# The gates' second products, two pairs behind their first, in a hybrid pooling and attention block

## The chip, the cores and the metric

The kernel runs on one core of one Trainium2 chip. Its time is the device time of one execution in microseconds (us). Before the change it is 1161.26 us, the median of 3 runs (1159.54 to 1161.93). One more execution was profiled; it took 1161.2 us, and its records span 1159.4 us. Engines are named as in the profile: PE is TensorE (PEld its weight loads), DVE VectorE, ACT ScalarE, POOL GpSimd, SP SyncE, which here only issues transfers (DMAs).

## The reference

One decoder block on x of 1024 tokens by 1024 channels, float32:

```
h = rmsnorm(x, g_mix_pre);  proj = h @ w_in + b_in
u_pool, q, k, v, gates = split(proj)            # 512, 512, 128, 128, 2 x 1024
# pooling mixer: 4 groups of 128 channels, windows 2, 4, 8, 16
y_pool = (mean of u over the last w tokens - u) @ w_pool[group] * pool_scale
# attention: 8 query heads on 2 key heads, blocks of 128 tokens, window 128, one sink logit a head
y_attn = softmax([q k^T / 8, sink]) v
merged = sigmoid(gates[:1024]) * (y_pool @ w_branch_pool) + sigmoid(gates[1024:]) * (y_attn @ w_branch_attn)
x = x + rmsnorm(merged @ w_out, g_mix_post)
ff = square(relu(rmsnorm(x, g_mlp_pre) @ w_up)) @ w_down
x = x + rmsnorm(ff, g_mlp_post)
```

## The kernel before, in words

**Products.** A float32 product is made of three matmuls of rounded halves: each operand is split into a high part (a cast, L101, on ScalarE) and the rest (a subtraction, L104, on VectorE); `split` does both. A `wh` tile holds such a split weight; there are six buffers of them (`wp`). A raw weight comes into a `st` buffer (three of them, 512 KB a load).

**Attention.** Tokens are cut into 8 blocks. The loop over n works on three blocks at a time: `attend_t(n)` transposes the probabilities of block n on TensorE, the softmax of block n+1 is finished, the scores of block n+2 are made (`score`, copied out of PSUM by ScalarE at L329; `score_prev` puts the previous block's scores in by VectorE at L336). `attend_v(n)` multiplies with v; its result is copied out by ScalarE at L392. `fill` puts matmuls of other work between: the rest of the q, k, v projection and then the pooling projection u (L576), groups 3, 2, 1, 0, in two halves each. VectorE scales each half (L579); ScalarE adds the bias when both are there (L582). The order of TensorE, VectorE and ScalarE in this loop is the order in which the code is written.

**Pooling.** `pool_in(gi)` makes the windowed mean of group gi on VectorE, in steps that the caller takes one by one: each doubling of the window is an add of shifted tiles (L605) and a short copy (L606); then the difference to u (L609 and two short rows, L610, L611); then a split into `ar` tiles. `pool_mix(gi)` is six matmuls (L624 to L626) in two `at` banks of PSUM; in the attention there are three such banks, which `attend_t` (two each) and `attend_v` use too.

**Gates.** The gate projection, 16 tiles of 128 channels, is computed pair by pair (8 pairs) with a Strassen-Winograd scheme: of 2x2 blocks (two channel tiles, two halves of the tokens) only 7 products are made instead of 8, each of 4 k-tiles and 3 passes, 12 matmuls (L480). `m1(p)` makes the first product in a bank `mm` (there are four) and has ScalarE copy the bank (L487); `m2(p)` accumulates the second product onto the same bank, and VectorE closes it (L718). Neither needs more than the x tiles of the attention stage. `rest(p)` makes the other five (names b6, b7, b5, and two that go into these banks again) and closes the two gate tiles: sigmoid on ScalarE, then out to DRAM (`z_dram`). These need tiles made from differences of x: `build_gate(kt)`, kt 0 to 3, loads two x tiles (L744, SyncE's queue), scales one on ScalarE (L746), makes four differences on VectorE (L749 to L752) and splits them (four casts, four subtractions). `prepare(p)` loads the raw weights of pair p and splits the two that m1 and m2 need; `operand(p, i)` makes the other five.

Behind the attention, before: for pairs 0 to 6 m1 and m2 are made one after the other, with pool_mix(2), (1), (0) and the four build_gate between; pairs 5 and 6 put their result (`f0`) to DRAM and get it back ahead of their rest(p); pair 7 makes its first two products inside rest(7). In this part only TensorE's order is the written one; where the other engines' rows stand is decided by a scheduler. The engines' queues, and SyncE's queue of transfers, are each worked off in order.

## Time and profile before

| | us |
|---|---|
| median of 3 runs | 1161.26 (1159.54 to 1161.93) |
| the profiled execution | 1161.2, span 1159.4 |
| TensorE busy, whole span | 1126.5 (97%) |
| VectorE, ScalarE busy | 821.2 (71%), 526.6 (45%) |
| TensorE busy from 165 to 235 us | 55.3 of 70 |

In the profile, L12 is line 12 of the kernel before. A row of the timeline reads: start in us, duration in us, engine, line, operation, output<-inputs, shape, how many, and in brackets how long the engine was idle before, and what ended that. ACTq and SPq rows are issues of transfers. A share of busy time over the whole span says little here: TensorE is full in all but two stages, the start and the one behind the attention, so the prediction goes by stages.

### The profile page before, as it was taken

The page shows a single profiled execution, that of the slowest core. Times are in us where ns is not written, and L with a number is a line of the kernel's source. Part 1 is how long each engine was busy: PE and PEld are TensorE (multiplying, and loading weights), DVE is VectorE, ACT ScalarE, POOL GpSimd, SP SyncE. Part 2 cuts the span into 40 slices and gives each one's busy share as a digit, 9 for nine tenths or more (in the row PEclk, how much of TensorE's full clock was granted, in tenths as well). Part 3 has the DMA queues.
Part 4 walks back from the last instruction along what each step waited for, and adds up shares of the span by engine and source line. Part 5 has one row for each costly group of instructions (what it writes and reads, how often), then busy time and mean ns, then how long its engine had stood idle before and what let it go on. Part 6 is the DMA issues. An engine that isn't in the chain of part 4 may idle for free.

```text
span 1159.4 us, 13966 instructions
## 1 busy us (share of the span) xinstructions
PE 1126.5 (97%) x5202; PEld 928.9 (80%) x5202; DVE 821.2 (71%) x1209; ACT 526.6 (45%) x912; POOL 64.3 (6%) x110
## 2 busy tenths in 40 slices
PE   7999988799999999999999999999999999999997
PEld 6888867578888888888788888888888888888885
DVE  7667887977854595666998766666647945446886
ACT  7465555543432233464655544444444345344342
POOL 3433100000000050000000000000000000000000
PEclk9999999799999999999999999999999999999999
DMA  7100214645346453233255434343688665432662
GB/s 260 64 1 19 91 57 179 237 145 198 139 174 217 138 205 129 109 127 145 92 200 209 165 144 164 140 162 145 248 290 312 206 204 175 130 104 73 201 194 96
DMA packets 67028, 182.22 MB, mean 157 GB/s; under 512 B 6288, under 2 KB 6288, under 8 KB 66960
## 3 DMA queue, kind: packets, MB, share of 16 engines
q1 hardware_dynamic: 60912, 159.83, 39.8%
q10 hardware_dynamic: 6048, 21.50, 4.7%
q8 instruction: 41, 0.67, 0.2%
q14 instruction: 27, 0.22, 0.1%
HBM read 129.92 MB, written 51.38 MB: 156 GB/s over the span
## 4 chain that ended last, share of the span: by engine, by line
PE 82%; DVE 8%; ACT 4%; DMA 2%; issue 2%; SPq 0%; DVEq 0%; ACTq 0%
PE mm L480 19%; PE at L480 15%; PE at L1199 14%; PE mm L1199 11%; PE mm L916 5%; PE mm L417 5%; PE mm L576 3%; PE mm L419 3%; PE mm L179 2%; PE at L388 1%; DVE wh L104 1%; PE sc L327 1%; PE at L916 1%; DMA st<-in_w_up_dram 1%; DVE T L104 1%
## 5 line engine op out<-in xcount | busy, mean ns | idle before, releaser
L1199 PE MATMUL at<-ar,wh 128*128 128x512 f32 x744 | 169.6, 389 | 0.0
L1199 PEld LDWEIGHTS at<-ar,wh 128*128 128x128 f32 x744 | 139.6, 188 | 29.3 <-DVE ar L104 0.4
L1199 PE MATMUL mm<-ar,wh 128*128 128x512 f32 x576 | 131.0, 389 | 0.0
L1199 PEld LDWEIGHTS mm<-ar,wh 128*128 128x128 f32 x576 | 108.1, 188 | 22.4
L101 ACT CAST wh<-st 128x512 fp32r<-128x512 f32 (+1 forms) x106 | 67.2, 642 | 124.3 <-PE mm L480 40.4
L104 DVE TENSOR_TENSOR wh<-raw,wh 128x1024 fp32r<-128x1024 f32 x53 | 64.8, 1223 | 82.3 <-ACT wh L101 82.3
L101 ACT CAST wh<-raw 128x1024 fp32r<-128x1024 f32 x53 | 55.8, 1053 | 132.0 <-PE at L1199 63.2
L104 DVE TENSOR_TENSOR wh<-st,wh 128x512 fp32r<-128x512 f32 (+1 forms) x106 | 82.9, 789 | 22.6 <-ACT wh L101 20.1
L480 PE MATMUL mm<-x,wh 128*128 128x512 f32 x240 | 62.9, 416 | 10.9 <-ACT g L487 7.7
L480 PE MATMUL mm<-gr,wh 128*128 128x512 f32 x300 | 72.1, 390 | 0.0
L480 PE MATMUL mm<-T,wx 128*128 128x512 f32 x288 | 67.6, 389 | 0.0
L480 PEld LDWEIGHTS mm<-x,wh 128*128 128x128 f32 x240 | 48.0, 202 | 23.5 <-ACT g L487 8.6
L480 PEld LDWEIGHTS mm<-gr,wh 128*128 128x128 f32 x300 | 56.1, 188 | 11.5
L480 PEld LDWEIGHTS mm<-T,wx 128*128 128x128 f32 x288 | 54.1, 188 | 11.2
L480 PE MATMUL at<-T,wx 128*128 128x512 f32 x252 | 59.1, 389 | 0.0
L480 PEld LDWEIGHTS at<-T,wx 128*128 128x128 f32 x252 | 47.3, 188 | 9.8
L104 DVE TENSOR_TENSOR ar<-B,ar 128x1024 fp32r<-128x1024 f32 x37 | 45.1, 1219 | 9.2 <-ACT ar L101 9.2
L576 PE MATMUL mm<-x,wh 128*128 128x512 f32 x192 | 47.1, 400 | 0.0
L480 PE MATMUL at<-gr,wh 128*128 128x512 f32 x183 | 44.7, 390 | 0.4 <-DVE z L508 0.4
L101 ACT CAST ar<-B 128x1024 fp32r<-128x1024 f32 x37 | 38.9, 1051 | 10.9 <-DMA B<-in_w_dn_dram 5.4
L576 PEld LDWEIGHTS mm<-x,wh 128*128 128x128 f32 x192 | 36.0, 191 | 8.1
L833 DVE TENSOR_TENSOR g<-g,mm 128x512 f32<-128x512 f32 x32 | 20.5, 683 | 28.5 <-PE mm L419 28.4
(356 smaller groups left out, 2190.9 us busy)
## 6 DMA issues: line engine op xcount, KB each, us to landing
raw<-f_dram SPq DMA_DIRECT2D x53, 512.0 KB, 3.7
f_dram<-g SPq DMA_DIRECT2D x30, 512.0 KB, 3.3
B<-in_w_dn_dram SPq DMA_DIRECT2D x24, 512.0 KB, 5.6
st<-in_w_up_dram SPq DMA_DIRECT2D x22, 512.0 KB, 3.6
st<-in_w_g_dram SPq DMA_DIRECT2D x18, 512.0 KB, 3.6
f_dram<-g ACTq DMA_DIRECT2D x17, 512.0 KB, 2.6
spill_dram<-z ACTq DMA_DIRECT2D x16, 512.0 KB, 3.1
g<-spill_dram SPq DMA_DIRECT2D x16, 512.0 KB, 4.3
```

The lines of the kernel that those rows point to most:

```text
L101: act.copy(hi, src)
L104: eng.tensor_tensor(lo, src, f32(hi), ALU.subtract)
L179: pe.matmul(bq, xs_[k][n // 4][:, xh, n % 4 * P:(n % 4 + 1) * P], wq[k][:, h, :], start=k == 0 and j == 0, stop=k == NK - 1 and j == 2)
L327: pe.matmul(sb[:, kv, i, :nk], qt[r, qx, m * P:(m + 1) * P], kx[r, k0:k0 + nk], start=j == 0, stop=j == 2)
L388: pe.matmul(yb.rearrange("p m q -> p (m q)"), v[:, vh, kv * HD:kv * HD + P], p[ph][:, 4 * kv:4 * kv + 4].rearrange("p i q -> p (i q)"), st ...
L417: pe.matmul(bs[th], whi[:, k, :], rhs(k, hl, th), start=k == 0 and hl == 0, stop=False)
L419: pe.matmul(bs[th], wlo[:, k, :], rhs(k, 0, th), start=False, stop=k == nk - 1)
L480: pe.matmul(b, w[:, wh, kt, :], xo[kt][:, xh, :], start=not after and kt == 0 and j == 0, stop=kt == 3 and j == 2, skip_group_check=after)
L576: pe.matmul(b, (whi, wlo)[h][:, k, :], xr(k, xh, th), start=j == 0, stop=j == len(mms) - 1)
L833: dve.tensor_tensor(z[:, sl], z[:, sl], bs[th], ALU.mult)
L916: pe.matmul(obs[n][dj], l, wos[k][whl][:, dj * 512:(dj + 1) * 512], start=k == 0 and hl == 0 and whl == 0, stop=k == NK - 1 and hl == 1)
L1199: pe.matmul(bs[t], fo[fh][:, k2, t * P:(t + 1) * P], wo_[wh][:, k2, :], start=not after and s2 == 0 and k2 == 0 and j == 0, stop=s2 == NS ...
```

## The change

Behind the attention all eight pairs get `first(p)` and `second(p)` early, and second(p) comes behind first(p+2). Three first products are then open at a time, in three of the four banks. f0 of pairs 2, 3, 4 lies in `g` buffers, that of pairs 5, 6, 7 goes to DRAM and back. In the attention loop the scores of block n+2 are made and copied ahead of half of the exponentials, and `score_prev` comes ahead of `attend_own`. The pooling's steps are spread by `pump(k, gi)`, which takes k steps of group gi: group 3's come earlier, group 2's in the last three blocks, and pool_mix(2) is made ahead of the last `attend_v`.

```diff
+        def pump(k, gi):
+            if gi not in sums:
+                sums[gi] = pool_in(gi)
+            for _ in range(k):
+                next(sums[gi], None)
...
             if n == 0:
                 softmax_exp(1, LOW)
+            if n + 2 < NT:
+                score(n + 2, 0)
             if n + 1 < NT:
                 softmax_exp(n + 1, HIGH)
             if n + 2 < NT:
-                score(n + 2, 0)
+                score_prev(n + 2, 0)
             attend_own(n)
-            if n + 2 < NT:
-                score_prev(n + 2, 0)
...
-            if n == NT - 1:
+            if n == 5:
+                pump(1, 3)
+            elif n == 6:
+                pump(1, 3)
+                pump(2, 2)
+            elif n == 7:
                 pool_mix(3)
+                pump(1, 2)
             fill(3.6)
...
-            for _ in range({4: 1, 5: 2, 6: 9}.get(n, 0)):
-                next(p3, None)
-            for _ in range({7: 3}.get(n, 0)):
-                next(p2, None)
+            if n in (4, 5):
+                pump(2, 3)
+            elif n == 6:
+                pump(2, 2)
+            elif n == 7:
+                pump(2, 1)
             fill(1e3 if n == NT - 1 else 4.1)
+            if n == 7:
+                pool_mix(2)
             attend_v(n)
...
+    def first(p):
+        gt.m1(p, bank("mm"), g32([S]) if 2 <= p < NHELD else None)
+    def second(p):
+        gt.m2(p)
+        if p >= NHELD:
+            nc.scalar.dma_start(z_dram[2 * p], gt.f0.pop(p))
...
-        for p in range(2):
-            gt.m1(p, bank("mm"))
-            gt.m2(p)
-        pool_mix(2)
-        finish(pool_in(1))
+        first(0)
+        first(1)
+        pump(9, 1)
         build_gate(0)
-        gt.m1(2, bank("mm"))
-        gt.m2(2)
+        first(2)
+        second(0)
+        gt.prepare(3)
+        pump(9, 0)
         pool_mix(1)
...
+        first(3)
+        second(1)
+        gt.prepare(4)
         build_gate(1)
...
         pool_mix(0)
+        first(4)
+        second(2)
+        gt.prepare(5)
         build_gate(2)
...
+        first(5)
+        second(3)
+        gt.prepare(6)
+        first(6)
+        second(4)
         build_gate(3)
...
+        gt.prepare(7)
+        first(7)
+        second(5)
+        second(6)
+        second(7)
```

TensorE, first gate products (`mm` are the banks, `x` and `wh` the operands). Before, the second product of bank mm_1922 follows its first at once:

```order
L480 MATMUL mm_1922<-x_192,wh_1898 128x512 x3
L480 MATMUL mm_1922<-x_234,wh_1898 128x512 x3
L480 MATMUL mm_1922<-x_275,wh_1901 128x512 x3
L480 MATMUL mm_1922<-x_317,wh_1901 128x512 x3
L480 MATMUL mm_1922<-x_358,wh_1901 128x512 x3
L480 MATMUL mm_1922<-x_400,wh_1901 128x512 x3
L480 MATMUL mm_1950<-x_109,wh_1906 128x512 x3
```

Now (bank mm_1939):

```order
L480 MATMUL mm_1939<-x_234,wh_1915 128x512 x3
L480 MATMUL mm_1954<-x_109,wh_1923 128x512 x3
L480 MATMUL mm_1954<-x_151,wh_1923 128x512 x3
L480 MATMUL mm_1954<-x_192,wh_1923 128x512 x3
L480 MATMUL mm_1954<-x_234,wh_1923 128x512 x3
L480 MATMUL mm_1997<-x_109,wh_1931 128x512 x3
L480 MATMUL mm_1997<-x_151,wh_1931 128x512 x3
L480 MATMUL mm_1997<-x_192,wh_1931 128x512 x3
L480 MATMUL mm_1997<-x_234,wh_1931 128x512 x3
L480 MATMUL mm_1939<-x_275,wh_1918 128x512 x3
```

Two first products of other banks have moved between the two halves.

VectorE, last two blocks of the attention, up to the L579 that closes the second half of group 1's projection (`t` and `u` are the pooling's tiles, u_1158 group 3's and u_1381 group 2's). Before:

```order
L605 TENSOR_TENSOR t_1740<-t_1655 128x1016
L606 COPY t_1740<-t_1655 128x8
L104 TENSOR_TENSOR wh_1898<-st_1896,wh_1898 128x512
L609 SCALAR_TENSOR_TENSOR u_1158<-t_1740,u_1158 128x1009
L610 TENSOR_TENSOR t_1740<-t_1740,cst 128x15
L104 TENSOR_TENSOR wh_1901<-st_1896,wh_1901 128x512
L611 TENSOR_TENSOR u_1158<-t_1740,u_1158 128x15
L104 TENSOR_TENSOR wh_1906<-st_1904,wh_1906 128x512
L104 TENSOR_TENSOR wh_1909<-st_1904,wh_1909 128x512
L104 TENSOR_TENSOR ar_1747<-u_1158,ar_1746 128x1024
L579 TENSOR_TENSOR u_1612<-mm_1671,rb_all 128x512
```

Now:

```order
L605 TENSOR_TENSOR t_1737<-t_1734 128x1022
L606 COPY t_1737<-t_1734 128x2
L104 TENSOR_TENSOR wh_1918<-st_1913,wh_1918 128x512
L605 TENSOR_TENSOR t_1756<-t_1737 128x1020
L606 COPY t_1756<-t_1737 128x4
L104 TENSOR_TENSOR wh_1923<-st_1921,wh_1923 128x512
L609 SCALAR_TENSOR_TENSOR u_1381<-t_1756,u_1381 128x1017
L610 TENSOR_TENSOR t_1756<-t_1756,cst 128x7
L104 TENSOR_TENSOR wh_1926<-st_1921,wh_1926 128x512
L611 TENSOR_TENSOR u_1381<-t_1756,u_1381 128x7
L579 TENSOR_TENSOR u_1618<-mm_1677,rb_all 128x512
```

Group 2's steps, which came behind that L579, now stand ahead of it, and the end of group 3's has moved further ahead.

SyncE's queue behind the attention (`st` raw gate weights, `y` the attention's result, `g` and `xr` the x tiles of build_gate; L744 is now L759 and L700 now L715). Before:

```order
L700 DMA spill_dram<-y_466 128x1024
L700 DMA spill_dram<-y_467 128x1024
L744 DMA g_2002<-in_xt_dram 128x1024
L744 DMA g_2004<-in_xt_dram 128x1024
L444 DMA st_2255<-in_w_g_dram 128x1024
L744 DMA g_2080<-in_xt_dram 128x1024
L744 DMA g_2082<-in_xt_dram 128x1024
L444 DMA st_2293<-in_w_g_dram 128x1024
L744 DMA xr_2197<-in_xt_dram 128x1024
```

Now:

```order
L759 DMA g_1976<-in_xt_dram 128x1024
L715 DMA spill_dram<-y_466 128x1024
L715 DMA spill_dram<-y_467 128x1024
L759 DMA g_1978<-in_xt_dram 128x1024
L444 DMA st_2207<-in_w_g_dram 128x1024
L444 DMA st_2264<-in_w_g_dram 128x1024
L759 DMA g_2090<-in_xt_dram 128x1024
L759 DMA g_2092<-in_xt_dram 128x1024
L759 DMA xr_2243<-in_xt_dram 128x1024
```

The weights of pair 7 (st_2264) have come ahead of the x tiles of build_gate(1).

## The prediction

> **What bounds the kernel now.** I read the busy time by stages first, then TensorE's timeline where it is not full, then the queues that its waits name.

> ```profile
> 165.00:235.00 70.00, 55.30 (x210) 42.95 (x208) 55.70 (x87) 36.30 (x59) 0.00 (x0) 0.88 0.52 188
> 210.00:235.00 25.00, 18.63 (x58) 14.56 (x58) 21.07 (x33) 12.96 (x23) 0.00 (x0) 0.73 0.68 249
> 258.00:300.00 42.00, 42.00 (x187) 34.80 (x186) 34.01 (x52) 17.70 (x24) 0.00 (x0) 1.00 0.48 179
> ```

> The columns are the stretch, then busy time of PE, PEld, DVE, ACT, POOL, then granted clock, DMA share and GB/s. From 258 us TensorE is full and stays so to the end but for odd microseconds; behind the attention (165 to 235) it is busy 55.3 of 70 us at a clock of 0.88. What the change can win is there. TensorE's timeline of that stage, with the waits in brackets:

> ```profile
> 76.32 0.39 PE L327 MATMUL sc<-klo,qt 64*128 64x256 f32 x2 [0.84 <-DVE den L357]
> ...
> 169.29 0.50 PE L624 MATMUL at<-ar,wpt 128*128 128x512 f32 x1 [3.68 <-ACT y L392]
> 171.96 8.14 PE L576 MATMUL mm<-x,wh 128*128 128x512 f32 x32
> 182.66 2.88 PE L480 MATMUL mm<-x,wh 128*128 128x512 f32 x12
> 186.21 5.74 PE L480 MATMUL mm<-x,wh 128*128 128x512 f32 x24 [0.68 <-ACT z L487]
> 192.74 3.06 PE L480 MATMUL mm<-x,wh 128*128 128x512 f32 x12 [0.79 <-ACT z L487]
> 195.63 0.39 PE L624 MATMUL at<-ar,wpt 128*128 128x512 f32 x1
> 196.99 2.88 PE L480 MATMUL mm<-x,wh 128*128 128x512 f32 x12
> 201.54 3.02 PE L480 MATMUL mm<-x,wh 128*128 128x512 f32 x12 [1.67 <-ACT z L487]
> 211.81 5.49 PE L480 MATMUL mm<-x,wh 128*128 128x512 f32 x12 [3.17 <-ACT g L487]
> 226.26 8.17 PE L480 MATMUL mm<-x,wh 128*128 128x512 f32 x24 [4.57 <-ACT g L487]
> 234.26 1.07 PE L480 MATMUL at<-gr,wh 128*128 128x512 f32 x4
> 235.17 5.70 PE L480 MATMUL mm<-x,wh 128*128 128x512 f32 x24
> ```

> Five times a second product waits for ScalarE's copy (L487) of the first product's bank, into which it accumulates: 0.68 + 0.79 + 1.67 + 3.17 + 4.57 = 10.88 us. Slow matmuls follow the longer waits: 12 take 2.88 at full clock and 5.49 after the wait of 3.17; 24 take 5.70, and 8.17 after the wait of 4.57. The copies are late since ScalarE's queue is in order and holds the casts of the gate operands ahead of them; the last one:

> ```profile
> 225.63 0.57 ACT L487 COPY g<-mm 128x512 f32<-128x512 f32 x1
> ```

> **The change, part by part.** I work against the profiled execution's own time, 1161.2 us (span 1159.4 and 1.8 around it); the median shown is 1161.26, so the same.

> *Second products two pairs later.* Two or more products of 12 matmuls now stand between a first product and its second. The row from 258 on counts 187 matmuls in 42.00 us, 0.225 each (a few records may be missing), so a product is 2.7 us. Pair 7's two products, now in the stage behind, are among those that come forward:

> ```profile
> 338.42 2.88 PE L480 MATMUL mm<-x,wh 128*128 128x512 f32 x12
> ...
> 343.86 2.88 PE L480 MATMUL mm<-x,wh 128*128 128x512 f32 x12
> ```

> A copy then has 5.4 us or more, against a worst wait of 4.57. I take all five waits as gone: 10.88 us, 0.16 each for the pipe's drain (a 2.88 group starts its follower after 2.72), 0.8, and the slow matmuls after them: 0.04 + 0.18 + 0.14 + 2.61 + 2.47 = 5.4. Together 17.1. The cover gone, the last wait and its slow clock alone are 7.0; bounds 10 to 17.1. Pair 7's products leave the later stage at the price they have here, so they cancel. Its result now goes to DRAM and back as those of pairs 5 and 6 do: one store on ScalarE's queue, one load on SyncE's, under the five products, 13.6 us, that rest() does for each pair. Hidden; nothing.

> *Scores ahead of the exponentials.* The copy of the scores moves ahead of four of eight exponentials:

> ```profile
> 71.96 3.08 ACT s L353 x16
> ```

> (chain of waits; 16 counts eight and their reads). Half is 1.54 us, more than the wait of 0.84 at 76.32; that wait goes. All later loops of the attention show no wait of TensorE, so 0.84 in all, bounds 0 and 0.84.

> *Pooling steps ahead.* This part costs. Group 2's steps now stand on VectorE ahead of the L579 that closes the second half of group 1's projection. Behind that L579 hang in turn ScalarE's L582, the copy L392, and pool_mix(3), which needs the bank that L392 empties:

> ```profile
> 166.84 0.68 DVE L579 TENSOR_TENSOR u<-mm,rb_all 128x512 f32<-128x512 f32 x1
> 167.56 1.15 ACT L582 ACTIVATE u<-u,vec 128x1024 f32<-128x1024 f32 x1 [1.90 <-DVE u L579]
> 168.62 0.62 ACT L392 COPY y<-at 128x256 f32<-128x256 f32 x2
> ```

> This is the wait of 3.68. VectorE's rows price what goes in front, and what leaves:

> ```profile
> 141.04 1.29 DVE L104 TENSOR_TENSOR s<-at,s 128x512 fp32r<-128x512 f32 x2 [2.35 <-ACT s L101]
> 149.08 0.74 DVE L336 COPY_PREDICATED s<-cst,sc 128x512 f32<-128x512 uint32 x1 [1.69 <-ACT s L329]
> 151.39 1.22 DVE L605 TENSOR_TENSOR t<-t 128x1022 f32<-128x1022 f32 x1
> 153.93 0.68 DVE L579 TENSOR_TENSOR u<-mm,rb_all 128x512 f32<-128x512 f32 x1
> 175.28 1.21 DVE L605 TENSOR_TENSOR t<-u 128x1023 f32<-128x1023 f32 x1
> 179.14 0.69 DVE L104 TENSOR_TENSOR wh<-st,wh 128x512 fp32r<-128x512 f32 x1
> 179.74 1.21 DVE L609 SCALAR_TENSOR_TENSOR u<-t,u 128x1017 f32<-128x1017 f32 x1
> 180.87 0.68 DVE L579 TENSOR_TENSOR u<-mm,rb_all 128x512 f32<-128x512 f32 x1
> ```

> Added: three steps of group 2 (175.28 to 179.14: 3.9), its L609 (179.74 to 180.87: 1.1) and two short rows (0.2). Gone from there: two steps of group 3 (151.39 to 153.93: 2.5). One of these goes ahead of the L336 at 149.08 and pushes it by 1.3, since ScalarE's score copy waits behind another L579 in that chain; the other falls into the idle 2.35 us ahead of 141.04 and costs nothing. Net 5.2 - 2.5 + 1.3 = 4.0: pool_mix(3) waits 7.7 instead of 3.7. After the old wait, six matmuls and 32 lost 1.9 to the slow clock (169.29 to 171.96 against 195.63 to 196.99, and 8.14 against 7.4); after 3.17 and 4.57 it was 2.6 and 2.5. So 4.0 and 0.3 more: 4.3, bounds 0 (L579 no later) and 5.5.

> [...]

> *What is late next.* On the present clock (all of it shifts by the 0.84) pool_mix(3) starts at 173.3, the first gate product at 188.0 (as now 13.4 later, and pool_mix(2), now ahead of it, 1.4). From there 15 products of 2.72 and two mixes bring TensorE to the first b6 product of rest(0) at 231.5; I add 0.5 for pool_mix(0), whose operand is ready just late. That b6 product needs build_gate's tiles and pair 0's weight for it. Their last rows now on VectorE, and the loads (SPq, SyncE's issues) and scalings of x:

> ```profile
> 220.77 0.69 DVE L749 TENSOR_TENSOR g<-g 128x512 f32<-128x512 f32 x1
> 230.84 0.68 DVE L104 TENSOR_TENSOR wh<-ws,wh 128x512 fp32r<-128x512 f32 x1
> ...
> 184.61 1.92 SPq L744 DMA_DIRECT2D g<-in_xt_dram  x2
> 191.02 0.90 SPq L744 DMA_DIRECT2D g<-in_xt_dram  x2
> ...
> 208.46 0.33 SPq L444 DMA_DIRECT2D st<-in_w_g_dram  x1
> 208.89 0.90 SPq L744 DMA_DIRECT2D xr<-in_xt_dram  x2
> ...
> 191.06 1.15 ACT L746 ACTIVATE g<-g,vec 128x1024 f32<-128x1024 f32 x1 [1.17 <-DMA g<-in_xt_dram]
> 213.38 1.15 ACT L746 ACTIVATE xr<-xr,vec 128x1024 f32<-128x1024 f32 x1 [1.11 <-DMA xr<-in_xt_dram]
> ```

> Now kt=0's x goes out at 184.6 and is scaled from 191.06, and kt=1's goes out at 191.0. In the change kt=0's first load stands one place ahead of the y stores, so its scaling ends at about 193.7, only 1.5 later than now though the attention ends 5.3 later; but two weight loads stand ahead of kt=1's, and the second waits for a buffer that VectorE frees behind build_gate(0). Up to there VectorE has thirteen rows of 0.60 to 0.65, an L605 and an L609 of 1.14, three short ones of 0.15 and half a microsecond for a cast: 11.3, so those loads go out at 205 (bounds: 200, if the buffer is freed ahead of the tiles, and 208). Landing 4.5 later, as 208.89 to 213.38 shows, kt=1 is there at 210 and kt=3, two loads on, at 213; scaled at 214.2, it starts thirteen more rows of VectorE, 8.1, up to kt=2: 222.3. Nine loads of 0.52 MB follow each other from 205, of which kt=2's are the last; they end by 220 at the best rate of the page (312 GB/s), by 224 at the 249 of the second stage row above:

> ```profile
> GB/s 260 64 1 19 91 57 179 237 145 198 139 174 217 138 205 129 109 127 145 92 200 209 165 144 164 140 162 145 248 290 312 206 204 175 130 104 73 201 194 96
> ```

> So at the better rate VectorE is the later. From 222.3 it needs 10.8 us as now (220.77 to 231.5) and three more closings and splits, 1.9: 235. TensorE, there at 232, waits about 3.0. I add 0.3 for drains: 3.3, bounds 0 and 9.

> [...]

> Sum: 17.1 + 0.84 - 4.3 - 3.3 = 10.3 us won. 1161.2 - 10.3 = 1150.9. Behind it nothing is lost again: VectorE is busy 34 of 42 us in the next stage, and the order of work behind the gates is unchanged.

> **The rivals.**
> *The x loads decide (A).* They run at 249 GB/s or wait longer for buffers: kt=2 comes 3.8 later, b6 with it, and a wait above 3 brings the slow clock, 2.5. Gain 10.3 - 6.3 = 4.0: 1157. For it: the row at 208.46 shows a load that held the x loads behind it. Against: VectorE has work of its own until 222.
> *VectorE keeps up (B).* L579 comes no later, because idle time such as the 1.69 at 149.08 takes up the steps. Then 4.3 more: 1146.6. Against: VectorE has no other idle row between 149 and 167.
> *Slower (C).* If the three rounds of x (load 6.4 as from 184.61 to 191.06, scale 1.15, four VectorE steps 2.7, casts and splits 2.5) run one after another from 205, 38 us, build_gate ends at 243, not 231, and b6 starts 14 later than forecast, with 2.5 of slow clock: 1167. It decides once b6(0) starts after about 244. Against: the second and third round are loaded while the first is split.
> *It does nothing (D).* The copies stay late behind ScalarE's casts by more than 5.4 us and the longer pooling wait eats the rest: about 1161. Against: the worst copy begins 4 us late now.

> **How the numbers follow.** Forecast 0.50, A 0.21, B 0.13, C 0.10, D 0.06. About 0.2%, 2.3 us, is what a measurement of this kernel can tell from no change. Forecast, A and B are faster: 0.84; D is the same: 0.06; slower 0.10. The range 1144 to 1158 takes in A and B with their bounds and leaves out C, D and a little of the rest; the forecast's own is 1147 to 1155. Predicted: 1150.9.

> **What would show it.** No wait of an L480 second product for L487; pool_mix(3) waiting about 7.7 us for L392, slow matmuls behind it; the wait of 0.84 gone; the first b6 product (at<-gr,wh) near 233.5 with all sixteen gate products but one ahead of it, and a wait of 2 to 4 for VectorE or ScalarE there; kt=1's x issued near 205. Wrong if pool_mix(3) starts at 169 or behind 176, if L487 waits remain, or if b6 starts behind 240.

## The result, and the profile after

The changed kernel takes 1152.2 us (median of 4 executions, 1151.14 to 1153.24), the kernel before beside it 1160.8 (4 executions, 1159.54 to 1161.93): the ratio is 0.9926, with an interval of 0.9909 to 0.9943, and 8.6 us are won. The forecast was 1150.9, so 10.3 won. The profiled execution took 1151.14 us, its span is 1149.3. Medians, ranges and ratios, here and below, leave out three executions that took about 1590 us and more.

Busy time by stages of the changed kernel, with the columns of the same view of before (the stretch, then PE, PEld, DVE, ACT, POOL, granted clock, DMA share, GB/s):

```profile
165.00:235.00 70.00, 60.86 (x252) 48.95 (x253) 53.65 (x85) 36.55 (x59) 0.00 (x0) 0.94 0.55 196
210.00:235.00 25.00, 22.33 (x94) 17.74 (x94) 23.30 (x38) 12.59 (x22) 0.00 (x0) 0.96 0.66 237
258.00:300.00 42.00, 42.00 (x187) 34.76 (x187) 36.66 (x57) 16.93 (x24) 0.00 (x0) 1.00 0.58 204
```

TensorE was busy 55.30 of 70 us at a clock of 0.88 behind the attention; now it is 60.86 at 0.94. Between 210 and 235, where the longest waits stood, it is 22.33 of 25 instead of 18.63. The stage from 258 on is as full as it was. TensorE's timeline of the changed kernel, with its waits in brackets:

```profile
57.97 3.75 PE L179 MATMUL mm<-wh,x 128*128 128x512 f32 x15 [0.24 <-ACT rb_all L403]
...
162.79 1.03 PE L370 MATMUL at<-cst,s 128*128 128x128 f32 x8
170.72 0.80 PE L624 MATMUL at<-ar,wpt 128*128 128x512 f32 x1 [6.89 <-ACT y L392]
...
173.44 8.16 PE L576 MATMUL mm<-x,wh 128*128 128x512 f32 x32
...
185.52 11.04 PE L480 MATMUL mm<-x,wh 128*128 128x512 f32 x48
...
204.48 0.50 PE L625 MATMUL at<-ar,wpt 128*128 128x512 f32 x1 [0.76 <-DVE ar L104]
...
205.74 24.66 PE L480 MATMUL mm<-x,wh 128*128 128x512 f32 x108
233.07 3.55 PE L480 MATMUL at<-gr,wh 128*128 128x512 f32 x7 [2.67 <-ACT wh L101]
236.82 3.02 PE L480 MATMUL mm<-x,wh 128*128 128x512 f32 x12 [0.21 <-ACT z L487]
...
251.69 2.20 PE L480 MATMUL mm<-gr,ar 128*128 128x512 f32 x9
```

Products run in one piece, 48 and 108 matmuls long, where five waits for L487 stood; 0.21 us is all that is left of these. Two long waits remain: pool_mix(3) for L392, 6.89 instead of 3.68, and the first b6 product of rest(0) (at<-gr,wh), 2.67. The same marks of before:

```profile
59.22 3.75 PE L179 MATMUL mm<-wh,x 128*128 128x512 f32 x15 [0.24 <-ACT rb_all L403]
...
164.57 1.03 PE L370 MATMUL at<-cst,s 128*128 128x128 f32 x8
...
252.56 2.37 PE L480 MATMUL at<-gr,wh 128*128 128x512 f32 x9 [0.36 <-DVE z L508]
...
262.26 2.20 PE L480 MATMUL mm<-gr,ar 128*128 128x512 f32 x9
```

Two marks divide the span. The first is attend_t(7) (L370); the second is the first of pair 1's three products from `ar` weights (mm<-gr,ar), behind the five of pair 0: 251.69 in the change. In before these three are interrupted by others, and the third begins at 262.26. In one piece the first would begin 5.44 earlier; but pair 7's two products, also 5.44, are still to come there and are done in the change. So 262.26 is the mark of before for the same work. What lies behind it confirms that: 1159.4 - 262.26 = 897.1 us in before, 1149.3 - 251.69 = 897.6 in the change.

Thus of the 10.1 us between the two spans, 1.25 stood already at the row at 59 (57.97 against 59.22), in code that the change does not touch; it is a difference between executions: this one of before has a stretch of slow clock from 43.7 on (18 matmuls of L179 take 5.94 us there, 4.37 in the change). From there to L370 0.53 is won, between the marks 97.69 - 88.90 = 8.79, and behind them 0.47 is lost. That is 8.85 from the change, beside 8.6 between the medians.

### The profile page after: what moved, and what is told of

It reads as the page before. It is cut to its first block, busy times and chain, and to the rows that moved or that the text cites. A ratio compares the mean times of both kernels' runs of the same rounds, so it can differ in the third digit from the quotient of the medians.

```text
span 1149.3 us, 13969 instructions
## 1 busy us (share of the span) xinstructions
PE 1121.2 (98%) x5202; PEld 925.8 (81%) x5202; DVE 819.5 (71%) x1209; ACT 525.2 (46%) x912; POOL 64.8 (6%) x110
## 4 chain that ended last, share of the span: by engine, by line
PE 85%; DVE 8%; DMA 3%; ACT 2%; issue 1%; SPq 0%; DVEq 0%; ACTq 0%
PE mm L480 18%; PE at L480 16%; PE at L1223 14%; PE mm L1223 11%; PE mm L940 5%; PE mm L417 5%; PE mm L179 3%; PE mm L419 3%; PE mm L576 2%; PE at L188 1%; PE sc L179 1%; DVE wh L104 1%; PE at L388 1%; PE sc L327 1%; PE at L940 1%
## 5 line engine op out<-in xcount | busy, mean ns | idle before, releaser
L101 ACT CAST wh<-st 128x512 fp32r<-128x512 f32 (+1 forms) x106 | 67.0, 641 | 125.4 <-PE mm L480 35.3
L104 DVE TENSOR_TENSOR wh<-raw,wh 128x1024 fp32r<-128x1024 f32 x53 | 64.8, 1222 | 82.7 <-ACT wh L101 82.7
L101 ACT CAST wh<-raw 128x1024 fp32r<-128x1024 f32 x53 | 55.8, 1053 | 133.3 <-PE at L1223 62.7
L104 DVE TENSOR_TENSOR wh<-st,wh 128x512 fp32r<-128x512 f32 (+1 forms) x106 | 82.9, 789 | 22.5 <-ACT wh L101 20.1
L480 PE MATMUL mm<-gr,wh 128*128 128x512 f32 x300 | 72.0, 390 | 0.0
L480 PE MATMUL mm<-T,wx 128*128 128x512 f32 x288 | 67.6, 389 | 0.0
L480 PEld LDWEIGHTS mm<-gr,wh 128*128 128x128 f32 x300 | 56.1, 188 | 11.5
L480 PEld LDWEIGHTS mm<-T,wx 128*128 128x128 f32 x288 | 54.1, 188 | 11.2
L480 PE MATMUL at<-T,wx 128*128 128x512 f32 x252 | 59.1, 389 | 0.0
L480 PE MATMUL mm<-x,wh 128*128 128x512 f32 x240 | 55.8, 390 | 0.2 <-ACT z L487 0.2
L480 PEld LDWEIGHTS at<-T,wx 128*128 128x128 f32 x252 | 47.3, 188 | 9.8
L480 PEld LDWEIGHTS mm<-x,wh 128*128 128x128 f32 x240 | 45.0, 188 | 10.1 <-ACT z L487 0.8
L104 DVE TENSOR_TENSOR ar<-B,ar 128x1024 fp32r<-128x1024 f32 x37 | 45.0, 1217 | 7.7 <-ACT ar L101 7.5
L480 PE MATMUL at<-gr,wh 128*128 128x512 f32 x183 | 46.2, 399 | 2.7 <-ACT wh L101 2.7
L576 PE MATMUL mm<-x,wh 128*128 128x512 f32 x192 | 47.4, 400 | 0.1
L480 PEld LDWEIGHTS at<-gr,wh 128*128 128x128 f32 x183 | 35.0, 193 | 10.9 <-ACT wh L101 3.1
L101 ACT CAST ar<-B 128x1024 fp32r<-128x1024 f32 x37 | 38.9, 1050 | 9.3 <-DMA B<-in_w_dn_dram 4.9
L576 PEld LDWEIGHTS mm<-x,wh 128*128 128x128 f32 x192 | 36.0, 191 | 8.6 <-ACT wh L101 0.5
```

What stands on the lines that cost most here:

```text
L101: act.copy(hi, src)
L104: eng.tensor_tensor(lo, src, f32(hi), ALU.subtract)
L480: pe.matmul(b, w[:, wh, kt, :], xo[kt][:, xh, :], start=not after and kt == 0 and j == 0, stop=kt == 3 and j == 2, skip_group_check=after)
L576: pe.matmul(b, (whi, wlo)[h][:, k, :], xr(k, xh, th), start=j == 0, stop=j == len(mms) - 1)
```

## The experiments

Each kernel ran beside the kernel before on the same chip, in three groups; the medians of before there were 1159.7, 1159.5 and 1161.2. The change itself was timed only in the group of the result, so a kernel is best compared with it by what each wins over its own before. Line numbers in the gates stage differ a little from kernel to kernel.

**The loop alone**: the change's attention loop with the gates of before.

```diff
...
-        first(0)
-        first(1)
+        for p in range(2):
+            gt.m1(p, bank("mm"))
+            gt.m2(p)
         pump(9, 1)
         build_gate(0)
...
```

> The kernel before with the change's attention loop alone (scores ahead, pooling spread); the gates' products as before. Theory: the wait of 0.84 for the scores goes, pool_mix(3) waits 3 to 4 us longer, the L487 waits stay at about 11; 1 to 4 us slower than before, 1162 to 1165. Rival (the loop's edits bring a good part of the gain): 1150 to 1158.

Measured: 1164.94 (1163.94 to 1165.5), ratio 1.0044 (1.0028 to 1.006), 5.3 us slower than before. The waits of TensorE (us in total, times, longest):

```profile
PE mm L480 <- ACT g L487: 7.9, 2, 6.4
PE at L624 <- ACT y L392: 6.9, 1, 6.9
...
PE mm L480 <- ACT z L487: 5.5, 3, 3.7
```

The longer wait for L392 comes from the loop, with or without the new gates; and the gates' waits for L487, 13.4 in all, are even longer than the 10.88 of before.

**The gates alone**: the change's gates behind the loop of before.

```diff
...
+    finish(p2)
...
         first(0)
         first(1)
-        pump(9, 1)
+        pool_mix(2)
+        finish(pool_in(1))
         build_gate(0)
...
```

> The gates stage as in the change, the attention's loop as before (group 2's three steps behind group 3's, pool_mix(2) between the second and third first product). Theory, the parts add up: the loop alone lost 5.2 us (1164.94 against 1159.71), the change won 8.6, so the gates alone win about 13.8: 1144 to 1149, with the wait of pool_mix(3) for L392 back at about 3.7 us and no wait of a second product for L487. Rival, the loop's later attention is not what costs in the gates: within 2 us of the change, 1150 to 1154.

Measured: 1146.44 (1144.9 to 1148.16), ratio 0.9884 (0.9862 to 0.9905): 13.1 us won. The parts add up to within 1 us: by medians +5.3 and -13.1 make -7.8, where the change has -8.6; by ratios +0.44% and -1.16% make -0.72%, where it has -0.74%. TensorE's timeline, then SyncE's issue of kt=1's x:

```profile
163.33 1.03 PE L370 MATMUL at<-cst,s 128*128 128x128 f32 x8
168.04 0.80 PE L624 MATMUL at<-ar,wpt 128*128 128x512 f32 x1 [3.68 <-ACT y L392]
...
204.85 24.66 PE L480 MATMUL mm<-x,wh 128*128 128x512 f32 x108
229.35 2.20 PE L480 MATMUL at<-gr,wh 128*128 128x512 f32 x9
...
245.72 2.20 PE L480 MATMUL mm<-gr,ar 128*128 128x512 f32 x9
```

```profile
188.95 0.90 SPq L744 DMA_DIRECT2D g<-in_xt_dram  x2
```

The wait for L392 is back at 3.68, and the b6 products stand right behind the 108 matmuls: no wait. So the wait of 2.67 in the change is no price of the gates' new order by itself. But two things differ here: the attention ends earlier, and kt=1's x goes out 25.6 us behind L370 (188.95 - 163.33), ahead of pair 7's weights; in the change it stands behind them and goes out 40.4 behind L370 (203.18 - 162.79). Which of the two counts is asked by the last runs below.

**Second products at once**: the change with each second(p) right behind first(p).

```diff
         first(0)
+        second(0)
         first(1)
+        second(1)
         pump(9, 1)
         build_gate(0)
         first(2)
-        second(0)
+        second(2)
...
```

> The changed kernel with each second gate product put right behind its first again (all eight pairs early, pooling spread as in the change). Theory (the spacing is the gain): the waits of TensorE for the copy L487 come back, about 9 to 11 us in all with 4 to 6 us of slow clock, the wait at the first b6 product shrinks by up to 4 since TensorE comes later; 1159 to 1166 us. Rival (the gain is from the pooling spread and from pair 7's products coming early, the spacing only moves a wait): L487 waits return but b6 comes no later, 1151 to 1155.

> The change with each second product right behind its first, for its profile. Theory: waits of L480 second products for L487 of 10 to 16 us in all, as the loop alone had with the gates of before (13.4), and 12 to 17 us lost with the slow clock behind them: near 1164. Rival, the price is elsewhere: L487 waits under 6 us.

Measured: 1163.87 (1162.52 to 1167.64), ratio 1.0042 (1.0027 to 1.0057), 4.2 us slower than before, where the change is 8.6 faster; the execution with the profile took 1163.69, and between the two marks it is 12.6 us longer than the change (table below). Its waits, and one row of its timeline:

```profile
PE mm L480 <- ACT g L487: 7.2, 3, 5.9
...
PE mm L480 <- ACT z L487: 5.4, 3, 3.6
```

```profile
228.14 8.30 PE L480 MATMUL mm<-x,wh 128*128 128x512 f32 x24 [5.85 <-ACT g L487]
```

12.6 us of waits for L487, and slow matmuls behind the long ones (24 take 8.30, in the change 5.60). The two pairs between first and second product take all of that away.

**The scores alone**: on the kernel before, only the scores ahead of the exponentials.

```diff
+            if n + 2 < NT:
+                score(n + 2, 0)
             if n + 1 < NT:
                 softmax_exp(n + 1, HIGH)
             if n + 2 < NT:
-                score(n + 2, 0)
+                score_prev(n + 2, 0)
             attend_own(n)
-            if n + 2 < NT:
-                score_prev(n + 2, 0)
```

> The kernel before with one edit: the scores of the later round and their copy ahead of the exponentials. Theory: the wait of 0.84 us of the scores product for VectorE's den is gone, no wait of that kind takes its place, and 0.8 us is won: 1159 on this chip, if the kernel before is near 1160. Rival: the wait moves to another product of the loop, 1160.

Measured: one execution, 1160.07. The wait of 0.84 for den is gone from the trace and none has come in its place in the loop (behind it the wait for L508 is 1.35 instead of 0.36). A gain of that size can't be told from no change in one time; the row says that the wait goes, the time does not say more.

**Group 2's steps behind pool_mix(3)**: the change with the early steps of group 2 taken out of the loop, and pool_mix(2) again behind attend_v(7).

```diff
             elif n == 6:
                 pump(1, 3)
-                pump(2, 2)
             elif n == 7:
                 pool_mix(3)
-                pump(1, 2)
...
-            elif n == 6:
-                pump(2, 2)
             elif n == 7:
-                pump(2, 1)
+                pump(9, 2)
             fill(1e3 if n == NT - 1 else 4.1)
+            attend_v(n)
             if n == 7:
                 pool_mix(2)
-            attend_v(n)
+                pump(2, 1)
```

> The changed kernel with group 2's pooling steps behind pool_mix(3) again, and pool_mix(2) behind the last attend_v; group 3's steps stay early. Theory (the longer wait of pool_mix(3) is a real loss of the change): L579 of group 1's second half comes about 5 us earlier, the wait for L392 falls from 6.9 to 2 to 3 us, and the whole is 2 to 5 us faster than the change, 1147 to 1150. Rival (the wait only moves: VectorE pays for group 2 later and the first b6 product waits instead): L392's wait falls, the wait at b6 grows to 6 or more, 1151 to 1154.

> Group 2's steps behind pool_mix(3) once more, now timed beside the variant with kt=1's x late, on one chip. Theory: 1140 to 1142 if the kernel before is near 1160.

Measured: 1140.22 (1139.63 to 1141.81), ratio 0.9834 (0.9817 to 0.9852), and on another chip 1142.19 (1141.05 to 1143.31), ratio 0.9846 (0.9828 to 0.9864). That is 19.5 and 19.0 us below before, 10.4 to 10.9 more than the change wins, where the theory expected 2 to 5; it is the best of these kernels. TensorE's timeline, then VectorE's:

```profile
164.11 1.03 PE L370 MATMUL at<-cst,s 128*128 128x128 f32 x8
...
166.22 0.50 PE L624 MATMUL at<-ar,wpt 128*128 128x512 f32 x1 [0.25 <-DVE s L104]
...
200.49 24.65 PE L480 MATMUL mm<-x,wh 128*128 128x512 f32 x108
224.98 2.20 PE L480 MATMUL at<-gr,wh 128*128 128x512 f32 x9
...
241.30 2.20 PE L480 MATMUL mm<-gr,ar 128*128 128x512 f32 x9
```

```profile
161.16 1.22 DVE L104 TENSOR_TENSOR ar<-u,ar 128x1024 fp32r<-128x1024 f32 x1
162.30 0.68 DVE L579 TENSOR_TENSOR u<-mm,rb_all 128x512 f32<-128x512 f32 x1
...
169.65 1.22 DVE L605 TENSOR_TENSOR t<-u 128x1023 f32<-128x1023 f32 x1
```

The wait for L392 is not 3.7 but nothing, the slow clock behind it is gone, and so is the wait at b6. VectorE shows why. In before the last doubling of group 3 and its L609 stood late, and L579 came 2.3 us behind L370's start (166.84 - 164.57). In the change group 3's steps are out of the way earlier, but group 2's have come in: L579 comes 5.5 behind (168.27 - 162.79). Here neither stands there: L579 comes right behind the split of `ar`, 1.8 ahead of L370 (162.30 - 164.11), and group 2's first step, at 169.65, no longer stands ahead of it. Four splits of gate weights (2.5 us), which stood among those steps in the other two, have moved behind L579 as well. Of the 11.7 us won between the two marks against the change (table below), 8.5 come from pool_mix(3) and the slow clock behind it and 5.1 from b6; 1.9 are lost again, since pool_mix(2) now waits 0.77 and pool_mix(0) 0.40 and 0.76. Half of the rearranging, group 3's part, was worth more than the whole.

**SyncE's queue in written order**, on the change and on the kernel just shown.

```diff
...
-    with tc.manual_schedule(engines={mybir.EngineType.PE}):
+    with tc.manual_schedule(engines={mybir.EngineType.PE, mybir.EngineType.SP}):
```

> The changed kernel with SyncE's queue in written order behind the attention, so that the x tiles of build_gate(1) go out ahead of the weights of pairs 5, 6, 7. Theory (the x loads, held behind a weight load that waits for a buffer, set the wait at the first b6 product): kt=1's x goes out 8 us or more earlier than at 203, VectorE's idle times of 3.4 and 1.4 us for L761 go, the b6 wait of 2.7 and the slow matmuls behind it go; 3 to 5 us faster than the change, 1147 to 1149.5. Rival (VectorE's own rows set it, as the prediction's sum took it): b6 waits 2 or more still, 1151 to 1153.

> Group 2's steps behind pool_mix(3) as in the run with that name (1140.2), and SyncE's queue in written order too. That run has kt=1's x on the queue at 189.8 and no wait at b6, so there is nothing left for the order of SyncE to win. Theory: 1139 to 1143, no wait at the first b6 product above 1 us. Rival, the order of SyncE is worth its 2 us here as well: 1137 to 1138.5.

The change: 1149.95 (1149.35 to 1151.22), ratio 0.9917 (0.9901 to 0.9933), some 2 us below the change's median and 1.1 more won over before, less than the theory wanted; its interval overlaps the change's, so the times don't tell the two apart. SyncE's issue of kt=1's x in the change and with this edit:

```profile
203.18 0.96 SPq L759 DMA_DIRECT2D g<-in_xt_dram  x2
```

```profile
192.64 0.95 SPq L759 DMA_DIRECT2D g<-in_xt_dram  x2
```

TensorE's timeline with the edit:

```profile
164.83 1.03 PE L370 MATMUL at<-cst,s 128*128 128x128 f32 x8
...
220.02 0.73 PE L480 MATMUL mm<-x,wh 128*128 128x512 f32 x2 [1.55 <-ACT wh L101]
221.30 13.44 PE L480 MATMUL mm<-x,wh 128*128 128x512 f32 x58 [0.55 <-DVE wh L104]
...
236.12 1.90 PE L480 MATMUL at<-gr,wh 128*128 128x512 f32 x7 [0.39 <-DVE wh L104]
...
251.71 2.20 PE L480 MATMUL mm<-gr,ar 128*128 128x512 f32 x9
```

The wait of 2.67 has become 1.55 + 0.55 + 0.39, now for the casts of the gate weights, whose loads have moved back. Between the marks this execution is 2.0 us shorter than the change: 1.7 at these waits, whose slow clock is gone, and 1.1 at pool_mix(0), which no longer waits, less 0.8 for a longer slow clock behind pool_mix(3) (32 matmuls of L576 take 9.01 us, 8.16 in the change). On the other kernel the written order wins nothing: 1142.39 (1140.74 to 1145.32), ratio 0.9851 (0.9827 to 0.9875).

**kt=1's x late**: group 2's steps behind pool_mix(3), SyncE's queue in written order, and the weight loads of pairs 5 to 7 ahead of kt=1's x.

```diff
...
         gt.prepare(4)
+        for p in (5, 6, 7):
+            gt.load(2 * p)
         build_gate(1)
```

> Group 2's steps behind pool_mix(3), but SyncE's queue in written order with the weight loads of pairs 5, 6 and 7 ahead of kt=1's x, as pairs 6 and 7 stand in the change. It asks whether the run at 1140.2 lost its wait at the first b6 product because the attention ends earlier or because kt=1's x stood ahead of a weight load that waits for a buffer. Theory, the load decides: kt=1's x goes out at about 201 instead of 189.8, the first b6 product comes 32.6 later as in the change (203.2 to 235.7), at 234 instead of 225, with slow matmuls behind the wait: 1148 to 1152. Rival, the attention's end decides: no wait there, 1140 to 1143.

> Group 2's steps behind pool_mix(3) and kt=1's x behind the weight loads of pairs 5 to 7, beside the same without that. In the profiles of the first runs, from the attention's last step to pair 0's b1 product, it is 80.06 against 77.19 us: theory, the later x costs 2.9 of the 11.7 us that separate that kernel from the change, so 2 to 4 us above the run beside it. Rival, within 1 us of it: x's place costs nothing, and the attention's earlier end gives all.

Measured: 1144.18 (1142.21 to 1145.39), ratio 0.986 (0.9836 to 0.9883); and beside the kernel without that 1144.0 (1142.7 to 1145.85), ratio 0.986 (0.984 to 0.988), against 1142.19. SyncE's issue of that x, without and with the edit, then TensorE's timeline with it:

```profile
190.53 0.90 SPq L756 DMA_DIRECT2D g<-in_xt_dram  x2
```

```profile
194.52 0.90 SPq L757 DMA_DIRECT2D g<-in_xt_dram  x2
```

```profile
162.81 1.03 PE L370 MATMUL at<-cst,s 128*128 128x128 f32 x8
...
225.25 2.48 PE L481 MATMUL at<-gr,wh 128*128 128x512 f32 x7 [1.81 <-DVE wh L104]
...
242.84 2.20 PE L481 MATMUL mm<-gr,ar 128*128 128x512 f32 x9
```

From L370's row to the x it is 31.7 us with the edit (194.52 - 162.81) and 26.1 without (190.53 - 164.44, the L370 of that run); in the change it is 40.4 (203.18 - 162.79). So the edit moves x by 5.6 (6.4 in the first pair of runs), not by the 11 that the theory wanted, and neither forecast of the first run came true: a wait of 1.81 comes back at b6 with slow matmuls behind it (seven take 2.48). Two things in the expectations are wrong: 235.7 for b6 in the change is the row's start with its wait added, the row starts at 233.07; and the second mark is pair 1's product, not pair 0's b1. The second pair of medians is 1.8 apart, just short of the theory's 2 to 4, and the intervals overlap; the trace makes it 2.5 between the marks (table below). The edit against the same kernel in written order, where kt=1's x goes out at 180.12, 16.9 behind L370, is 1.8 by medians (1144.18 against 1142.39) and 1.1 between the marks. How late kt=1's x is does count, then, but in these kernels it is worth 1 to 3 of the 10 to 12 us. Most came from the attention's earlier end, which also moves the x.

The stage between the two marks, for all of these (L370's start, the second mark, the difference, and the rest of the span):

| kernel | L370 | mark | between | behind |
|---|---|---|---|---|
| before | 164.57 | 262.26 | 97.69 | 897.1 |
| the change | 162.79 | 251.69 | 88.90 | 897.6 |
| loop alone | 163.32 | 265.52 | 102.20 | 897.7 |
| gates alone | 163.33 | 245.72 | 82.39 | 897.4 |
| second products at once | 163.18 | 264.65 | 101.47 | 897.2 |
| change, SyncE written | 164.83 | 251.71 | 86.88 | 897.7 |
| group 2 behind | 164.11 | 241.30 | 77.19 | 897.3 |
| the same, SyncE written | 163.19 | 242.13 | 78.94 | 897.6 |
| group 2 behind, second chip | 164.44 | 241.99 | 77.55 | 897.3 |
| the same, x late, second chip | 162.81 | 242.84 | 80.03 | 898.1 |

Whatever was edited, what is won or lost is won or lost between the marks; behind them it is 897 to 898. Here the parts add up less neatly than by ratios: +4.5 for the loop and -15.3 for the gates make -10.8, and the change has -8.8. The 2.0 that are missing have the size of a wait like that at b6, which the change has and neither part has alone; the medians can't tell so little.

## Why the prediction was right, and where it was not

The sum, term by term (us, gains positive; measured by the rows shown):

| step | predicted | measured |
|---|---|---|
| second products two pairs later | +17.1 | +17.7 |
| wait for L508 of before, gone too | 0 | +0.7 |
| scores ahead of the exponentials | +0.84 | +0.84, less 0.3 elsewhere in the loop |
| pooling steps ahead | -4.3 | -3.3 |
| pool_mix(0) | 0.5, not in the sum | -1.2 |
| first b6 product | -3.3 | -5.1 |
| behind the stage | 0 | -0.5 |
| net | +10.3 | +8.85 by the trace, 8.6 by medians |

**Second products.** Right, in mechanism and size. The waits for L487 are gone to 0.21, and with them the drains and the slow clock. Counted against matmuls that follow each other without a break (0.2267 us each, as the 108 of group 2 behind that take 200.49 to 224.98; 2.72 a product), the rows of before lose 17.7 at and behind the five waits and 0.7 at the wait for L508 (0.36, with its drain); the change loses 1.2 at pool_mix(0) and 5.1 at b6. With the 3.3 that the attention ends later, 18.4 - 1.2 - 5.1 - 3.3 = 8.8 is what the marks show. With the second products at once the change is 12.6 us longer between the marks: 12.6 of waits and 5 to 6 of slow clock and drains, less some 6 at pool_mix(0) and b6 that a later TensorE does not lose.

**Pooling.** The chain was as told: group 2's steps ahead of L579, then L582, L392, pool_mix(3).

```profile
168.27 0.68 DVE L579 TENSOR_TENSOR u<-mm,rb_all 128x512 f32<-128x512 f32 x1
```

```profile
168.98 1.15 ACT L582 ACTIVATE u<-u,vec 128x1024 f32<-128x1024 f32 x1 [9.70 <-DVE u L579]
170.04 0.63 ACT L392 COPY y<-at 128x256 f32<-128x256 f32 x2
```

The wait grew by 3.2, not 4.0, and the slow clock behind it by 0.1. (The 0.3 that is lost elsewhere in the loop stands just ahead: the 34 matmuls of L576 before L370 take 8.37 us, 7.97 in before; why is not shown.) But the step put only these 4.3 on the account of the pooling, and took before's own 3.68 and its slow clock as given. The run with group 2's steps behind pool_mix(3) shows that all of it, before's share too, hung on what stands ahead of that L579.

**The first b6 product: the term that was mis-sized.** With the 2.1 us by which everything stood earlier in the profiled execution (1.25 + 0.84), the forecast put kt=1's x at 203, VectorE's last operand at 233 and TensorE at 230. In the profile kt=1's x goes out at 203.18, and VectorE has:

```profile
209.63 0.69 DVE L764 TENSOR_TENSOR g<-g 128x512 f32<-128x512 f32 x1 [3.41 <-ACT g L761]
...
221.09 0.68 DVE L764 TENSOR_TENSOR g<-g 128x512 f32<-128x512 f32 x1
...
231.67 0.69 DVE L456 TENSOR_TENSOR ws<-ws,st 128x512 f32<-128x512 f32 x1
...
233.48 0.68 DVE L104 TENSOR_TENSOR wh<-ws,wh 128x512 fp32r<-128x512 f32 x1
```

TensorE stood there from 230.4 and went on at 233.07; the wait was 2.67, forecast 3.0. What failed is the step "I add 0.3 for drains": behind the wait seven matmuls took 3.55 us. Nine at full clock take 2.20 (the row at 229.35 of the gates alone), so seven 1.75, and 1.8 more went to the slow clock, which the prediction counted only in rival A and only above a wait of 3. The rest of the 5.1 are a wait of 0.21 for L487 and 0.4 of drain and start. A slip is in the sum as well: the 0.5 of pool_mix(0) was put into the time at which TensorE arrives at b6, which shortens the wait there, but not subtracted. It measured 0.76 of wait and 0.4 of drain and start. Together these are 3.0 us; the shortfall is only 1.5 by the trace, since the pooling cost 1.0 less than was put down and the waits of before were worth 1.3 more, while 0.8 was lost in the loop and behind the stage. That the errors offset each other is luck.

**The rivals.** A (the x loads decide) did not come true: the operand that was last at b6 is pair 0's weight sum, L456 and its cast, on a VectorE that is busy 23.30 of 25 us there; kt=2's x was there when VectorE reached it, as forecast. Still, VectorE stands idle 3.41 us for kt=1's scaled x, and with x earlier on the queue the long wait shrinks and splits up, with x later one appears. So A named a lever that the traces show, of 1 to 3 us; the times alone don't settle it. B (VectorE keeps up) is refuted by L579, 3.2 later against L370; C by b6 at 233; D by the missing L487 waits. In C's own sum 243 against 231 is 12 later, not 14. One question was missing among the rivals: whether the wait at b6 belongs to the gates' new order or to the attention's later end. The gates alone have no such wait, so it does not belong to the first by itself; an early attention with a late x has 1.81 of it, and how the rest divides between the attention's end and the place of x is not shown.

## What to carry to other kernels

When work is moved ahead on a busy engine, look first at which single row there sets free the bank or buffer that the bottleneck waits for, and price the move by what stands ahead of that row; here four short steps on the wrong side of one VectorE row were worth more than half of the main gain. Don't take a wait that exists before the change as given: here the rows that made it longer could be placed so that it vanished. Count a slow clock behind every wait of some 2 us, not only behind the long ones (of the waits measured behind the attention the shortest with one was 1.80 us, the longest without 1.67), and try a change of several parts by its parts.

## What the runs showed of the hardware

```profile
168.00:168.50 0.50, 0.00 (x0) 0.00 (x0) 0.50 (x3) 0.00 (x0) 0.00 (x0) 0.60 0.00 0
174.50:175.00 0.50, 0.50 (x2) 0.40 (x2) 0.24 (x1) 0.21 (x1) 0.00 (x0) 0.57 0.00 0
...
232.50:233.00 0.50, 0.00 (x0) 0.00 (x0) 0.50 (x2) 0.50 (x1) 0.00 (x0) 0.95 0.95 254
236.00:236.50 0.50, 0.50 (x2) 0.00 (x0) 0.00 (x0) 0.31 (x1) 0.00 (x0) 0.63 0.37 148
```

The first lasts from 168.1 to 174.93, 6.83 us; the second from 232.95 to 236.37, 3.42. Counted the same way it is 3.41 to 3.42 behind the waits of 1.80 and 1.81 (x late, first and second chip), 3.68 (before, and the gates alone) and 3.60 (second products at once), 6.83 behind 3.17 and 4.57 (before) and 5.85 (second products at once), and 10.24 behind 6.87 (SyncE written). The length of the wait does not fix the number of pieces: 6.83 follow the wait of 6.89 in the change, 10.24 that of 6.87 with SyncE written; and 6.83 follow 3.17 in before, where 3.41 follow 3.68. No slow clock follows the waits of 1.55 (SyncE written) and 1.67 (before). So of these waits none up to 1.67 and each from 1.80 on cost one such piece or more, and part of a piece lies inside the wait (in the change 168.1 to 170.72); the matmuls right behind it lost 1.8 us in the change (3.55 against 1.75, at b6) and 2.7 with the second products at once (8.30 against 5.60). A single long wait is not the whole condition: in the first profile of group 2 behind, eight matmuls of L402 at 57.17 take 1.92 us and the 15 of L179 at 58.91 take 4.16, behind waits of 0.7 and 0.47 alone; the change has the same two waits, 0.68 and 0.48, and there these take 1.04 and 3.75.
